# When the third pair's raw up weights are loaded in the second half of a gated MLP

## The chip, the cores and the metric

The kernel runs on one core of a Trainium2 chip. The metric is the device time of one execution in microseconds. The core has five engines that run their own instruction streams and meet through semaphores: TensorE (PE, with PEld for the loading of its weights), VectorE (DVE), ScalarE (ACT), GpSimd (POOL) and SyncE (SP), which here only issues transfers.

## The reference

One decoder layer on 2048 tokens of width 1024: conditioning, two kinds of attention, an output projection, a gated MLP with a causal convolution of width 3, and a final norm. The change touches the up projection of the MLP alone:

```python
h = rms_norm(x, g_mlp[l]) * (1.0 + scale_m) + shift_m
u = causal_depthwise_conv(h @ w_up[l], conv_w[l], conv_b[l])
u_gate, u_val = jnp.split(u, 2, axis=-1)
x = x + gate_m * ((jax.nn.silu(u_gate) * u_val) @ w_down[l])
```

`w_up` is 1024 x 5504 (2752 columns for the gate, 2752 for the value), all in float32.

## The kernel before

**Products.** Each float32 operand is split into a high part, rounded to float32r by ScalarE, and the rest, subtracted by VectorE or GpSimd (`split`, lines 44 to 46). A product is three matmuls: high by high, high by rest, rest by high (`product`, line 1313; its matmuls are recorded at L1315). Products are besides arranged in a fast scheme with seven products in place of eight for a 2 x 2 block product, so operands of h and of the weights are first combined by additions and subtractions.

**Halves and pairs.** The 2048 tokens are worked in two halves of 1024 (`sblk` 0 and 1). In each half the loop goes over 21 pairs of column blocks (128 columns of the gate and the same 128 of the value), and then over a rest of 64 and 64 columns. The first half takes the pairs in the order 0 to 20, the second in the order 2, 3, 0, 1, 4, 5 and so on. So the third pair of the second half is pair 0. The seven finished weights of pairs 2 and 3 were stored in the first half (`wus`), and the second half reads them back (`w_reload`, line 1248; L1251); the other pairs are made anew from the raw weights.

**h.** The second half needs its own operands of h. `load_h` (line 1164, L1167) reads each of four blocks j into a tile `xh`; `h_operands` (line 1169) makes seven operands of it, `op0` to `op6`, with VectorE subtracting (L1192, L1193, L1198, L1199) and `split` making the parts (L45 on ScalarE, L46 on VectorE). The seventh needs a scratch tile `t4` (L1199). The last of all, `obs[NK - 1][6]` with NK = 4, lies in a tile of its own, `op_s`. For the second half they are made while the first half's rest and the second half's first pair are running.

**Raw weights.** `load_pair` (line 1226) fetches the gate and the value columns of one pair from `w_up` into one tile of `raws()` (line 1208), two transfers of 512 KB on SP's queue (L1214). `w_operands` (line 1233) makes seven weights of it: GpSimd makes two combinations in tiles `ws` and one in place (L1237, L1238, L1239), and later a fourth in place (L1246); each is then split into a tile `wu` (L45, L46). The first weight needs no combination, the second needs L1239's.

**Buffers.** `raws()` and the tiles `xh` are allocated from the same three buffers (tag "xh"). `ws` and `t4` share three buffers (tag "ws"); `wu` has seven; accumulators, `snap`, `y` and `u` have their own small rings. A tile gets a buffer when its first instruction is ready and a buffer is free.

**The loop.** At step n the loop (from line 1469) asks for the raw weights of the pair two steps ahead (line 1471), takes the generator that makes the next pair's weights (`weights`, line 1465), and runs seven products over four blocks: 84 matmuls, in `pair_first` (line 1326) at n = 0 and in `pair` (line 1346) after that. `end_pair` (line 1431) then convolves the pair's two tiles `y` into `u` (`conv_tile`, line 1376), gates them and stores the result (`store_g`, line 1404). Two pairs 2k and 2k + 1 share a block `gs[k]`: the odd one's values are added there, by a transfer that accumulates (L1420, on GpSimd's queue), onto what the even one stored (L1415, L1416).

**What sets the order.** The kernel is written in a tile framework. It adds all semaphores, and a planner (`schedule_with_timeline_sim=True`) orders the instructions of each engine and queue ahead of time by its own estimate of when each is ready, with the order of the program as priority. In the stages of attention and output projection the kernel fixes parts of this order by hand (`fixed`, `issue_after`); in the loop of the up projection it doesn't.

Of the kernel before, what the change touches and what calls it, by code (L numbers as in the profile page):

```python
# [34 lines left out]
def kernel(ctx: ExitStack, tc: tile.TileContext, x, c, w_ada, b_ada, g_attn, w_in, b_fgate,  # L35
                      g_out_fox, g_out_sb, w_out, g_mlp, w_up, conv_w, conv_b, w_down, g_final, out):
    nc = tc.nc
# [3 lines left out]
    def f(t):  # L41
        return t.bitcast(F32)
# [62 lines left out]
    def drain(g):  # L105
        for _ in g:
            pass
# [116 lines left out]
    for r, src in ((R_GA, g_attn), (R_GM, g_mlp), (R_GF, g_out_fox), (R_GS, g_out_sb), (R_BA, b_ada)):  # L224
        n = src.shape[1] // P
# [600 lines left out]
    def attend_steps(u):  # L826
        kind, p, tb = u
        if kind == "fox":
            return sum(2 * (2 + 2 * tb + j2 + 1) for j2 in range(2)) + 1
        return sum(2 * (tb + 1 + 2 * tb + j2 + 1) for j2 in range(2)) + 1  # L830
# [199 lines left out]
    for i, u in enumerate(units):  # L1030
# [10 lines left out]
        n = attend_steps(u)  # L1041
# [34 lines left out]
    def chunk(u, c):  # L1076
        t, n, q = ORDER.get(u, TURN)[c]
        if (t, n) not in banks:
            banks[t, n] = bank(psc, "bc", 2) if u == 1 and t == 0 else bank(psd, "o", 4)
        with fixed():  # L1080
            out_matmuls(u, banks[t, n], t, n, q)
        return t, n, q
# [78 lines left out]
    NK = KT // 2  # L1161
    xhs = {}

    def load_h(sblk, j):
        xhs[j] = ho.tile([P, 2, SB], F32, name="xh", bufs=3)
        for i in range(2):
            nc.sync.dma_start(xhs[j][:, i], hms[sblk][:, j + i * NK])  # L1167

    def h_operands(j, sub):
        xh = xhs[j]  # L1170
        tt = ho.tile([P, 2, TB], F32, name="tt", bufs=1)
        t4 = wp.tile([P, TB], F32, name="t4", tag="ws", bufs=3)
        b11, b12 = xh[:, 0, 0:TB], xh[:, 0, TB:SB]
        b21, b22 = xh[:, 1, 0:TB], xh[:, 1, TB:SB]
        ops = obs[j] = [None] * 7

        def put(s, src):
            if j == 0:
                t = ho.tile([P, 2, TB], F32R, name=f"op{s}")
            elif j == NK - 1 and s == 6:  # L1180
                t = spare.tile([P, 2, TB], F32R, name="op_s")
            else:
                t = big4("op")
            split(t[:, 0], t[:, 1], src, nc.vector)
            ops[s] = t

        put(0, b11)
        yield
        put(2, b21)
        put(5, b22)  # L1190
        yield
        sub.tensor_sub(tt[:, 0], b22, b12)  # L1192
        sub.tensor_sub(b12, b12, b11)  # L1193
        yield
        put(4, tt[:, 0])
        put(3, b12)
        yield
        nc.vector.tensor_sub(tt[:, 1], b22, b12)  # L1198
        nc.vector.tensor_sub(t4, b21, tt[:, 1])  # L1199
        yield  # L1200
        put(1, tt[:, 1])
        yield
        put(6, t4)
        yield

    obs = {}

    def raws():
        return ho.tile([P, 2, KT, P], F32, name="wuraw", tag="xh", bufs=3)

    def load_up(raw, col_sets):
        at = 0
        for col, n in col_sets:
            nc.sync.dma_start(raw[:, :, at:at + n], w_up[:, col:col + n].rearrange("(k p) n -> p k n", p=P))  # L1214
            at += n
        return raw

    def w_split(s):
        w = w_tile()
        split(w[:, 0], w[:, 1], s, nc.vector)  # L1220
        return w

    def load_part(t, ci, v):
        return load_up(t[:, v], [(v * DFF + ci * P, P)])

    def load_pair(ci):
        t = raws()
        return load_part(t, ci, 0), load_part(t, ci, 1)

    def w_tile():  # L1230
# [2 lines left out]
    def w_operands(g, v, save=None):  # L1233
        a11, a12, a21, a22 = g[:, 0:NK], g[:, NK:KT], v[:, 0:NK], v[:, NK:KT]
        s3 = wp.tile([P, NK, P], F32, name="ws", tag="ws", bufs=3)
        s2 = wp.tile([P, NK, P], F32, name="ws", tag="ws", bufs=3)
        nc.gpsimd.tensor_sub(s3, a11, a21)  # L1237
        nc.gpsimd.tensor_add(a21, a21, a22)  # L1238
        nc.gpsimd.tensor_sub(s2, a21, a11)  # L1239
        for i, a in enumerate((a11, s2, a12, a21, s3, a12, a22)):  # L1240
            w = w_split(a)
            if save is not None:
                nc.sync.dma_start(wus[save][i], f(w).rearrange("p a k n -> p a (k n)"))
            yield w
            if i == 2:
                nc.gpsimd.tensor_sub(a12, a12, s2)  # L1246

    def w_reload(ci):
        for t in wus[ci]:
            w = w_tile()  # L1250
            nc.sync.dma_start(f(w).rearrange("p a k n -> p a (k n)"), t)  # L1251
            yield w
# [43 lines left out]
    for u in range(1, NU):  # L1296
        for c in range(8 if u == 1 else 0, 16):
            t, n, q = chunk(u, c)
# [22 lines left out]
    def y_tile():  # L1321
        return up_.tile([P, SB + 2], F32, name="y", bufs=3)
# [3 lines left out]
    def pair_first(ws, yg, yv, after):  # L1326

        banks = [bank(psd, "o", 4), bank(psd, "o", 4), bank(psd, "o", 4), bank(psd, "o", 4),
                 bank(psd, "t", 2), bank(psd, "t", 2), bank(psc, "bc", 2)]
        for j in range(NK):  # L1330
            for s in (1, 4, 6, 0, 2, 5, 3):
                product(banks[s], ws[s], obs[j][s], j, j == 0, j == NK - 1)
            if after is not None:
                after(j)
        b1, b6, b2, b5, b7, b3, b4 = banks
        p1, t, u3 = snap(), snap(), snap()
        nc.scalar.activation(p1, b1, AF.Copy)
        nc.vector.tensor_add(t, b6, p1)
        nc.vector.tensor_add(yg[:, T0], b2, p1)
        nc.vector.tensor_add(u3, b7, t)  # L1340
        nc.vector.tensor_add(t, b5, t)
        nc.vector.tensor_add(yv[:, T1], b5, u3)
        nc.vector.tensor_add(yg[:, T1], b3, t)
        nc.vector.tensor_add(yv[:, T0], b4, u3)
# [101 lines left out]
    soon, held = [], []  # L1446
    for sblk, order in enumerate(orders):
        after = None
        if sblk == 0:
            for j in range(1, NK):  # L1450
                if j == NK - 1:
                    load_h(0, j)
                drain(h_operands(j, nc.vector))
            ws = first["ws"]
            after = finish_last
            soon.append(load_pair(1))
        else:
            for j in range(NK):
                if j:
                    load_h(1, j)  # L1460
                drain(h_operands(j, nc.vector))
            for fn in held:
                fn()

        def weights(n):
            ci = order[n]
            return w_reload(ci) if sblk and ci in SAVE else w_operands(*soon.pop(0), ci if ci in SAVE else None)

        for n, ci in enumerate(order):
            if n + 2 < NFULL and not (sblk and order[n + 2] in SAVE):  # L1470
                soon.append(load_pair(order[n + 2]))
            if n == NFULL - 2:
                raw = load_up(raws()[:, 0], [(NFULL * P, REST), (DFF + NFULL * P, REST)])
            last_pair = n == NFULL - 1
            if not last_pair:
                nxt = weights(n + 1)
            elif sblk == 0:
                load_h(1, 0)
                back = w_reload(SAVE[0])
                nxt = islice(back, 5)  # L1480
            else:
                nxt = None
            yg, yv = y_tile(), y_tile()
            if n == 0:
                pair_first(ws, yg, yv, after)
                ws = list(nxt)
            else:
                ws = pair(ws, nxt, yg, yv)
            if last_pair and sblk == 0:
                held.append(lambda yg=yg, yv=yv, ci=ci: end_pair(ci, 0, yg, yv))  # L1490
            else:
                end_pair(ci, sblk, yg, yv)
        w1, w2 = w_split(raw[:, 0:NK]), w_split(raw[:, NK:KT])
        y = y_tile()
        a, b = bank_a(), bank_a()
        oa = [[obs[j][s] for s in (0, 2, 5, 3)] for j in range(NK)]
        for j in range(NK):
            product(a, w1, oa[j][0], j, j == 0, j == NK - 1)
        p1 = snap()
        nc.scalar.activation(p1, a, AF.Copy)  # L1500
        for j in range(NK):
            product(b, w1, oa[j][3], j, j == 0, False)
        for j in range(NK):
            product(a, w2, oa[j][1], j, False, j == NK - 1)
        nc.scalar.activation(y[:, T0], a, AF.Copy)
        for j in range(NK):
            product(b, w2, oa[j][2], j, False, j == NK - 1)
        nc.vector.tensor_add(y[:, T1], b, p1)
        if sblk == 0:
            held.append(lambda y=y: end_rest(y, 0))  # L1510
            ws = ws + list(back)
        else:
            end_rest(y, 1)
# [14 lines left out]
    for kp in range(PRE):  # L1528
        if kp % 2 == 0:
            pre = ho.tile([P, 2, 2, TB], F32, name="pre", tag="xh", bufs=3)  # L1530
        t = pre[:, kp % 2]
# [153 lines left out]
    for i in range(7):  # L1685
        nxt = {}
        kept = []
        for s in range(2):
# [4 lines left out]
            if left:  # L1693
                half, n = lefts[i]
# [68 lines left out]
```

## Time and profile before

| | us |
|---|---|
| runs | 2942.23, 2947.29, 2953.07 |
| median | 2947.29 |
| profiled execution, its time | 2943.39 |
| profiled execution, its span | 2941.4 |
| TensorE busy in the span | 2867.8 |
| granted clock, mean | 0.993 |

The span goes from the first instruction to the last. "Busy" is the time in which an engine works on an instruction; TensorE's instructions overlap, and their ends are modelled. The views used below are: busy time of each engine by stretches; who waited for whom; and the order of time, in which a row has its start, its length, engine, line, operation, tiles written and read, shapes, how many instructions were merged in it, and in brackets the engine's idle time before it and what ended that. For SP a row is the issue of transfers, not their landing. The second half of the up projection runs from about 2104 to 2495 us.

### The profile page before, as it was taken

Reading aid. Unit: us, or ns where it says so; the run is one execution under the profiler, and the core shown is the slowest. Engines: PE = TensorE matmul, PEld = TensorE weight load, DVE = VectorE, ACT = ScalarE, POOL = GpSimd, SP = SyncE. Lnnn points to the kernel's source line nnn. Section 1 sums busy time; section 2 is a strip of 40 time slices with the busy share of each in tenths; the row PEclk is TensorE's granted clock in tenths of the full one; section 3 lists DMA queues with packets and bytes.
Section 4 is the critical chain, followed back from the end, with each engine's and each line's share of the span. In section 5 each row is a group of like instructions: output and inputs, shape, how many; then the busy total and the mean of one; then the engine's idle time right before and its main releaser. Section 6 shows DMA issues by size and latency. Waiting matters only on the chain.

```text
span 2941.4 us, 45922 instructions
## 1 busy us (share of the span) xinstructions
PE 2867.8 (97%) x15772; PEld 2459.7 (84%) x15772; DVE 2179.5 (74%) x3464; ACT 1686.0 (57%) x3187; POOL 901.1 (31%) x967
## 2 busy tenths in 40 slices
PE   8999999999999999999999999999999999999998
PEld 7888888888988988888888788888788888888887
DVE  5787778877886656658843788888998888575476
ACT  5776767677776656658744554444444445433342
POOL 0431322243032423231213344444254543142200
PEclk8999999999999999999999999999999999999999
DMA  9749756867469794794537775554754444975644
GB/s 293 255 139 321 236 188 207 301 211 229 162 212 356 269 277 139 232 323 140 182 120 233 245 232 128 130 136 129 236 132 125 130 130 132 309 257 185 216 158 151
DMA packets 348346, 601.89 MB, mean 205 GB/s; under 512 B 34672, under 2 KB 178800, under 8 KB 348112
## 3 DMA queue, kind: packets, MB, share of 16 engines
q1 hardware_dynamic: 324208, 558.06, 57.7%
q0 software_dynamic: 10880, 20.97, 4.3%
q10 hardware_dynamic: 13024, 19.93, 1.9%
q8 instruction: 124, 2.03, 0.3%
q14 instruction: 110, 0.90, 0.1%
HBM read 420.77 MB, written 177.02 MB: 203 GB/s over the span
## 4 chain that ended last, share of the span: by engine, by line
PE 46%; DMA 3%; DVE 2%; SPq 1%; ACT 1%; issue 1%; POOL 0%; DVEq 0%; ACTq 0%; POOLq 0%
PE ps_o L1315 19%; PE ps_t L1315 7%; PE ps_o L1614 6%; PE ps_t L1614 3%; PE ps_bc L1614 3%; PE ps_o L912 1%; PE ps_pv L615 1%; DMA r<-rstd 1%; PE ps_bc L912 1%; PE ps_pt L606 1%; PE ps_o L1609 1%; DMA wo<-wos 1%; DMA hm<-hf_m 1%; SPq L895 1%; DVE op L46 1%
## 5 line engine op out<-in xcount | busy, mean ns | idle before, releaser
L1315 PE MATMUL ps_o<-op,wu 128*128 128x512 f32 x2592 | 608.0, 389 | 2.0 <-DVE snap L1366 1.5
L1315 PEld LDWEIGHTS ps_o<-op,wu 128*128 128x128 f32 x2592 | 486.2, 188 | 103.9 <-DVE snap L1366 1.9
L611 DVE TENSOR_TENSOR at<-ps_pt,at 128x512 fp32r<-128x512 f32 (+1 forms) x576 | 366.1, 652 | 100.2 <-ACT at L610 97.3
L636 DVE TENSOR_TENSOR_SCAN a<-r,a 128x512 f32<-128x512 f32 (+2 forms) x320 | 368.3, 1167 | 77.8 <-ACT a L631 39.9
L342 PE MATMUL ps_pj<-hp,w_qk 128*128 128x512 f32 x1512 | 411.2, 403 | 14.5 <-DMA hp<-hs 12.9
L610 ACT ACTIVATE at<-ps_pt 128x512 fp32r<-128x512 f32 (+1 forms) x576 | 318.5, 576 | 139.1 <-PE ps_pt L606 123.1
L615 PE MATMUL ps_pv<-at,V 128*128 128x256 f32 x2216 | 386.8, 292 | 9.3 <-DVE at L611 4.2
L615 PEld LDWEIGHTS ps_pv<-at,V 128*128 128x128 f32 x2216 | 320.9, 190 | 39.8 <-DVE at L611 11.4
L342 PEld LDWEIGHTS ps_pj<-hp,w_qk 128*128 128x128 f32 x1512 | 275.4, 190 | 71.0 <-DMA hp<-hs 16.2
L45 ACT ACTIVATE wu<-wuraw 128x512 fp32r<-128x512 f32 x204 | 128.9, 632 | 248.5 <-PE ps_o L1315 190.1
L596 PE MATMUL ps_qk<-K,Q 128*128 128x512 f32 (+2 forms) x640 | 265.7, 416 | 5.6 <-ACT a L631 3.3
L413 PE MATMUL ps_pj<-w_v,hp 128*128 128x256 f32 (+1 forms) x1536 | 236.6, 288 | 2.1 <-DVE hp L422 1.6
L597 PE MATMUL ps_qk<-K,Q 128*128 128x512 f32 (+2 forms) x640 | 235.7, 369 | 0.0
L1315 PE MATMUL ps_t<-op,wu 128*128 128x512 f32 x888 | 220.8, 390 | 1.0 <-DVE op L46 1.0
L413 PEld LDWEIGHTS ps_pj<-w_v,hp 128*128 128x128 f32 x1536 | 209.0, 189 | 10.9 <-DVE q L373 1.5
L630 ACT ACTIVATE r<-ps_qk 128x512 f32<-128x512 f32 (+2 forms) x320 | 173.1, 541 | 58.2 <-PE ps_qk L597 55.5
L46 DVE TENSOR_TENSOR wu<-wuraw,wu 128x512 fp32r<-128x512 f32 x204 | 189.6, 930 | 18.1 <-ACT wu L45 16.7
L1315 PEld LDWEIGHTS ps_t<-op,wu 128*128 128x128 f32 x888 | 166.4, 188 | 36.5 <-DVE op L46 1.8
L606 PE MATMUL ps_pt<-edge,a 128*128 128x128 f32 x1088 | 185.1, 274 | 8.4 <-DVE a L636 7.8
L1614 PE MATMUL ps_o<-op 128*128 128x512 f32 x840 | 191.5, 389 | 0.0
L1614 PEld LDWEIGHTS ps_o<-op 128*128 128x128 f32 x840 | 157.7, 188 | 32.7
L679 ACT ACTIVATE p<-p,mn 128x128 f32<-128x128 f32 (+15 forms) x128 | 153.9, 1203 | 53.3 <-DVE mn L675 52.2
(342 smaller groups left out, 5237.6 us busy)
## 6 DMA issues: line engine op xcount, KB each, us to landing
hp<-hs SPq DMA_DIRECT2D x224, 512.0 KB
wuraw<-in_w_up_dram SPq DMA_DIRECT2D x80, 512.0 KB
ra<-g SPq DMA_DIRECT2D x136, 256.0 KB
rb<-in_w_down_dram SPq DMA_DIRECT2D x108, 256.0 KB
g<-u SPq DMA_DIRECT2D x80, 256.0 KB
hs<-hp SPq DMA_DIRECT2D x32, 512.0 KB
hp<-in_w_ada_dram SPq DMA_DIRECT2D x32, 512.0 KB
qk_fox<-q SPq DMA_DIRECT2D x32, 512.0 KB
```

The source lines that it names most:

```text
L46: (lo_engine or nc.gpsimd).tensor_sub(lo, src, f(hi))
L342: nc.tensor.matmul(acc, w[kt][:, a, n], h[:, bb], start=kt == 0 and i == 0, stop=kt == KT - 1 and i == 2)
L413: nc.tensor.matmul(av[:, t * width:(t + 1) * width], hts[kt][:, a, tok], w[1][kt][:, bb, 0:width], start=kt == 0 and m == 0, stop=kt == KT ...
L596: nc.tensor.matmul(b[:, :cw], Q[:, hl, 0, qcols], K[:, hl, :cw], start=True, stop=False)
L597: marks.append(nc.tensor.matmul(b[:, :cw], Q[:, hl, 1, qcols], K[:, hl, :cw], start=False, stop=True).ins)
L606: nc.tensor.transpose(b[:, i * P:(i + 1) * P], blk(kts[kk], qi), ident)
L610: copies = [nc.scalar.activation(at[:, 0, lo:], b[:, lo:], AF.Copy).ins, nc.vector.tensor_sub(at[:, 1, lo:], b[:, lo:], f(at[:, 0, lo:])).ins]
L611: nc.vector.tensor_sub(at[:, 1, lo:], b[:, lo:], f(at[:, 0, lo:])).ins]
L615: m = nc.tensor.matmul(o[:, 0:2 * P], V[kt // 4][:, kt % 4, hl, :], rhs, start=first and kk == 0 and w == 0, stop=last and kk == 1 and w == 1)
L636: nc.vector.tensor_tensor_scan(rev, r[:, 0:need][:, ::-1], rev, 0.0 if right[qi] is None else right[qi][:, 0:1], ALU.mult, ALU.add)
L1315: nc.tensor.matmul(b, w[:, p, j], o[:, q], start=first and i == 0, stop=last and i == 2, skip_group_check=True)
L1614: nc.tensor.matmul(b, a[:, p, t * P:(t + 1) * P], w[:, q], start=first and i == 0, stop=last and i == 2, skip_group_check=True)
```

## The change

`load_pair` gets a second argument. Where it is given, GpSimd first copies 128 x 2 numbers, the first of the operand's high and of its low part in each partition, into the raw weights' tile, onto the first number of the gate's and of the value's part; the transfers that follow write over them. Since the copy reads the operand and the transfers overwrite what it wrote, the transfers wait for the copy, and the copy waits for the operand. The loop gives the argument at the first step of the second half alone, where the third pair (pair 0) is asked for, and the operand is `op_s`, the last of h. Nothing that is computed changes.

```diff
-    def load_pair(ci):
+    def load_pair(ci, after=None):
         t = raws()
+        if after is not None:
+            nc.gpsimd.tensor_copy(t[:, :, 0, 0:1], f(after[:, :, 0:1]))
         return load_part(t, ci, 0), load_part(t, ci, 1)
...
             if n + 2 < NFULL and not (sblk and order[n + 2] in SAVE):
-                soon.append(load_pair(order[n + 2]))
+                soon.append(load_pair(order[n + 2], obs[NK - 1][6] if sblk and n == 0 else None))
```

## The prediction

> **What bounds the kernel now.** I read four views in this order: the page's table of engines, the busy time of each engine by stretches around the start of the second half, TensorE's waits there, and then the order of time of each engine and queue in the same 60 us.
>
> ```profile
> span 2941.4 us, 45922 instructions
> PE 2867.8 (97%) x15772; PEld 2459.7 (84%) x15772; DVE 2179.5 (74%) x3464; ACT 1686.0 (57%) x3187; POOL 901.1 (31%) x967
> ```
> ```profile
> 2100.00:2120.00 20.00, 18.58 (x80) 14.45 (x79) 19.93 (x25) 10.39 (x17) 6.35 (x5) 1.00 0.71 219
> 2120.00:2140.00 20.00, 19.96 (x88) 16.15 (x87) 16.65 (x22) 8.07 (x12) 6.68 (x6) 1.00 0.62 205
> 2140.00:2160.00 20.00, 20.00 (x90) 16.54 (x89) 18.70 (x23) 9.43 (x14) 8.97 (x8) 1.00 0.38 119
> 2160.00:2180.00 20.00, 20.00 (x90) 16.57 (x89) 20.00 (x24) 9.13 (x13) 11.65 (x9) 1.00 0.78 198
> ...
> 2400.00:2500.00 100.00, 100.00 (x443) 82.80 (x442) 84.91 (x103) 48.12 (x67) 38.66 (x31) 1.00 0.44 126
> ...
> 2800.00:2941.40 141.40, 130.82 (x578) 108.03 (x576) 98.12 (x183) 50.62 (x114) 0.00 (x0) 0.98 0.46 154
> ```
>
> Behind the stretch come PE, PEld, DVE, ACT and POOL busy, then clock, DMA share and GB/s. TensorE sets the time: 2867.8 of 2941.4 us. The change can act from about 2104 us on, where the second half's third pair is loaded. There TensorE is idle for 1.42 us (20.00 less 18.58), then full; the next idle time of size is 10.6 us at the very end (141.40 less 130.82). So 1.42 us is what an edit at this place can win directly.
>
> ```profile
> PE ps_t L1315 <- DVE op L46: 1.0, 1, 1.0
> PE ps_o L1315 <- DVE op L46: 0.5, 1, 0.5
> ```
> ```profile
> 2118.41 0.73 PE L1315 MATMUL ps_t<-op,wu 128*128 128x512 f32 x2 [0.95 <-DVE op L46]
> 2119.62 6.88 PE L1315 MATMUL ps_o<-op,wu 128*128 128x512 f32 x29 [0.47 <-DVE op L46]
> 2126.33 0.84 PE L1315 MATMUL ps_bc<-op_s,wu 128*128 128x512 f32 x3
> 2127.22 0.73 PE L1315 MATMUL ps_o<-op,wu 128*128 128x512 f32 x2
> 2127.79 2.91 PE L1315 MATMUL ps_t<-op,wu 128*128 128x512 f32 x12
> ```
>
> Both waits (0.95 and 0.47 us) are for operands of h that VectorE makes. What holds VectorE up shows when its rows are laid beside GpSimd's.
>
> ```profile
> 2101.10 1.28 DVE L1386 SCALAR_TENSOR_TENSOR u<-y,conv,u 128x1024 f32<-128x1024 f32 x1
> ...
> 2107.72 0.69 DVE L46 TENSOR_TENSOR op<-tt,op 128x512 fp32r<-128x512 f32 x1
> ...
> 2112.66 2.32 DVE L1386 SCALAR_TENSOR_TENSOR u<-y,conv,u 128x1024 f32<-128x1024 f32 x1
> 2114.90 1.78 DVE L46 TENSOR_TENSOR op<-xh,op 128x512 fp32r<-128x512 f32 x1
> 2116.60 1.76 DVE L46 TENSOR_TENSOR op<-tt,op 128x512 fp32r<-128x512 f32 x1
> ...
> 2122.91 0.69 DVE L46 TENSOR_TENSOR op_s<-t,op_s 128x512 fp32r<-128x512 f32 x1
> ```
> ```profile
> 2107.26 1.18 POOL L1381 COPY halo<-y 128x2 f32<-128x2 f32 x1 [11.97 <-DVE y L1508]
> ...
> 2112.61 1.28 POOL L1237 TENSOR_TENSOR ws<-wuraw 128x512 f32<-128x512 f32 x1 [4.04 <-DMA wuraw<-in_w_up_dram]
> 2113.97 2.16 POOL L1238 TENSOR_TENSOR wuraw<-wuraw 128x512 f32<-128x512 f32 x1
> 2116.21 1.61 POOL L1239 TENSOR_TENSOR ws<-wuraw 128x512 f32<-128x512 f32 x1
> 2123.68 1.29 POOL L1237 TENSOR_TENSOR ws<-wuraw 128x512 f32<-128x512 f32 x1 [5.87 <-DVE op_s L46]
> ...
> 2126.28 0.19 POOL L1378 COPY y<-halo 128x2 f32<-128x2 f32 x1
> ```
>
> While GpSimd does the third pair's three combinations (1.28 + 2.16 + 1.61 = 5.05 us), three VectorE instructions take 2.32, 1.78 and 1.76 us, against 1.28 and 0.69 undisturbed: 1.04 + 1.09 + 1.07 = **3.2 us of delay** just before the operands for which TensorE waits. op_s is complete at 2123.60 (2122.91 + 0.69).
>
> **The change, part by part.** The loads concerned, on SP's queue, and the first use of the third pair's weights:
>
> ```profile
> 2104.82 1.01 SPq L1214 DMA_DIRECT2D wuraw<-in_w_up_dram  x2
> ...
> 2107.87 2.99 SPq L1214 DMA_DIRECT2D wuraw<-in_w_up_dram  x2
> 2116.09 4.61 SPq L1251 DMA_DIRECT2D wu<-wus  x5
> ...
> 2122.24 1.42 SPq L1214 DMA_DIRECT2D wuraw<-in_w_up_dram  x2
> 2123.75 4.83 SPq L1251 DMA_DIRECT2D wu<-wus  x2
> ```
> ```profile
> 2126.53 0.63 ACT L45 ACTIVATE wu<-wuraw 128x512 fp32r<-128x512 f32 x1 [3.65 <-PE ps_o L1315]
> ...
> 2127.21 0.30 PEld L1315 LDWEIGHTS ps_o<-op,wu 128*128 128x128 f32 x2 [0.46 <-ACT wu L45]
> ```
> ```profile
> 2130.69 10.43 PE ps_o L1315 x46
> ```
>
> By the loop's order the three pairs of L1214 loads are those of the third, fourth and fifth pair of the half; the L1251 loads bring the second pair's finished weights back. Nothing is removed. **Added** is one GpSimd copy of 128 x 2 numbers: the same shape costs 0.19 to 1.18 us here. GpSimd is idle 13.3 of 20 us between 2120 and 2140 (6.68 busy), so it lies beside other work; without that cover it delays at most the instruction behind it, a fourth pair's combination, by 1.2 us.
>
> **Moved** are two loads of 512 KB and what hangs on them. Load to first use took 2112.61 - 2104.82 = 7.8 us. If the loads keep their buffer and merely wait, they start at 2123.60 + 0.6 = 2124.2, GpSimd begins at 2132.0, and its three instructions end at 2137.0. The first weight needs no combination: its split (0.63 + 0.69 us, as the ACT and VectorE rows) is done at 2133.3; the second, made of the last combination, at 2138.3. When does TensorE need them? A matmul takes 10.43/46 = 0.227 us. After 2127.2 at least 84 - 29 = 55 matmuls of the second pair are left (the x29 row cannot hold more of it): 12.5 us, so the need is at 2139.7, and for the second weight 12 matmuls later, at 2142.4. Margins: 6.4 and 4.1 us. What is late next is the two matmuls at 2127.22, which are already of the third pair and fill a gap: without them TensorE waits from 2127.2 to 2127.8, 0.6 us. The 1 MB that now stands in the busiest stretch costs 1.05 MB / 205 GB/s = 5.1 us to whatever is behind it, at worst 1.0 us beyond the second weight's margin. So, if the change does what it says: at best **-1.4 us** (both waits gone), with the filler gone -0.8, and from the other side -1.42 + 1.42 (waits unchanged) + 0.6 + 1.0 + 1.2 = **+2.8 us**. I take -0.8, since the margins hold.
>
> The rows say that one engine's instruction stretches beside the other's by about 1 us each. [...]
>
> **But does it do that?** The wait is tied to a buffer, not to GpSimd. Three buffers are shared by the loads of h and the raw weights, and they fall free at 2104.82, 2107.87 and 2122.24, all before op_s. Nothing in the code keeps the fourth pair's load from the buffer that the third leaves, and the order of this loop is the planner's, which takes what is ready: that third pair's matmuls stand at 2127.22, amid the second's, shows it. Then the fourth pair is loaded at 2104.82, finds the same two free buffers for its combinations (now its L1237 at 2123.68 waited for the one under op_s), and the same three instructions meet VectorE at 2112.6. The pairs have changed places, and the stall of 1.42 us stays. I hold this likeliest: **no change, +0 to +1.2 us** for the copy.
>
> The profiled execution took 2943.39 us (2941.4 of span and 2.0 around it), 3.9 below the median of 2947.29; all sums are differences, so forecast and rivals are put on the median: 2947.3 + 0 gives **2947**.
>
> **The rivals.**
>
> *It does what it says* (chance 0.24): the buffer is kept for the third pair. For it: VectorE's 3.2 us lie directly ahead of the stall. Against it: the free buffer. 2947.3 - 0.8 = 2946.5.
>
> *The wait takes its place in a queue* (0.10): SP holds the delayed load ahead of the five L1251 loads of 2116.09. They would start at 2124.2 and land, by the 7.8 us of the L1214 loads, at 2132.0, where TensorE has work of the first pair only until 2123.5 (if 12 of the x29 row are the second pair's first product, 17 are the first's: 2119.62 + 17 x 0.227): 8.5 us, 2955.8. Against it: SP now puts the loads of 2107.87 ahead of these reloads although they belong to a later pair, so queues are filled by readiness.
>
> *The third pair is left out in the cold* (0.22, the slower side): fourth, fifth and sixth pair take all three buffers before op_s is made, the third gets one only when a pair is used up, and its load competes with each later one. The fourth pair's gated product must then wait in its buffer (of three) for the third's sums, since the two share a block of g. Price: a pair whose raw weights come without lead costs load, combinations and split: 7.8 + 5.05 + 1.3 = 14.2 us. Now the third pair has a lead of 2127.21 - 2104.82 = 22.4 us; it decides once a lead falls under 14.2. One such pair gives 2961.5, two 2975.7. For it: VectorE has no reserve to catch up at once (20.00 of 20.00 in 2160 to 2180). Against it: TensorE is full from 2127 on even after that squeeze.
>
> *A luckier order* (0.04): the 10.6 us at the end shrink with the 1.42. Even all of both is 12.0 us, 2935; for over 14.7 us something would be needed that no row here shows.
>
> **How the numbers follow.** The forecast has 0.40. A measurement here can tell about 0.5%, 14.7 us, from no change. Forecast, does-as-it-says and queue (0.40 + 0.24 + 0.10) stay within that: 0.74. The cold third pair, 14.2 to 28.4 us, I count whole to slower: 0.22; the lucky order, generously, to faster: 0.04. The forecast's own range is the runs' scatter (2942.23 to 2953.07) with -1.4 and +2.8: 2941 to 2956. The range for 8 in 10 reaches to one lost lead and the scatter above it, 2961.5 + 5.8 = 2967, and 2 us lower than the scatter: 2939.
>
> **What would show it.** Right: in 2104 to 2128 TensorE again idles about 1.4 us behind L46 making op, three GpSimd instructions L1237 to L1239 stand before op_s, and the L1214 loads at about 2105 and 2108 are still there, with another pair's columns; the new copy stands on GpSimd after op_s. The rival is right if GpSimd is free of L1237 to L1239 from 2110 to op_s and the VectorE rows read 1.28 and 0.69. The queue shows as L1251 loads after the copy; the cold pair as TensorE idle for 5 us or more behind wu after 2130. Wrong altogether I am if TensorE's idle time after 2130 grows by over 15 us, or if its idle time before 2100 changes.

## The result, and the profile after

The changed kernel took 2952.11 us in the median of 20 runs (2948.12 to 2959.85); the kernel before, run beside it, 2947.84 (2942.12 to 2953.48, 20 runs). The medians differ by 4.3 us. The ratio is 1.0017 with a 95% interval of 1.0009 to 1.0025: by it about 5.0 us slower, between 2.7 and 7.4. That is less than 0.5%, but "no change" lies outside the interval. The profiled execution took 2955.03 us, 11.6 more than the profiled one of before, so more than half of that difference must be scatter, and the first question is where it arose.

**A measure for that.** Both traces hold 15772 TensorE matmuls. I subtract the start of the n-th matmul of the one from that of the n-th of the other and call the difference the lag (worked out from the trace's records). From the 10800th matmul to the 12000th, before the first instruction that the change touches, the lag of the changed kernel is constant at 6.80 us: scatter of the earlier stages. At the 12090th (2093.2 us in the trace of before) it is 6.88, at the 12270th 5.96, at the 12300th 11.34, and from the 12420th to the end 11.76. What the change does is what the lag gains from the 12090th to the 12600th (2211.5 us): **+4.9 us**, of one execution, against +5.0 by the timed ratio. It falls into a small gain, -0.9 us, and a loss of 5.8 us some 20 us later. In the rows of after everything behind line 1226 stands two lines lower (L1315 is now L1317), and 7 us are to be taken off their times to lay them beside those of before.

The gain first. VectorE and GpSimd ahead of op_s, and then GpSimd's next rows, after the change (in order of time):

```profile
2119.00 1.28 DVE L1388 SCALAR_TENSOR_TENSOR u<-y,conv,u 128x1024 f32<-128x1024 f32 x1
2120.20 0.68 DVE L46 TENSOR_TENSOR op<-xh,op 128x512 fp32r<-128x512 f32 x1
2120.80 0.68 DVE L46 TENSOR_TENSOR op<-tt,op 128x512 fp32r<-128x512 f32 x1
...
2126.03 0.69 DVE L46 TENSOR_TENSOR op_s<-t,op_s 128x512 fp32r<-128x512 f32 x1
```
```profile
2126.78 0.19 POOL L1229 COPY wuraw<-op_s 128x2 f32<-128x2 f32 x1 [11.87 <-DVE op_s L46]
2126.90 0.19 POOL L1380 COPY y<-halo 128x2 f32<-128x2 f32 x1
2139.11 1.29 POOL L1239 TENSOR_TENSOR ws<-wuraw 128x512 f32<-128x512 f32 x1 [12.02 <-DMA wuraw<-in_w_up_dram]
2140.48 2.15 POOL L1240 TENSOR_TENSOR wuraw<-wuraw 128x512 f32<-128x512 f32 x1
2142.71 2.14 POOL L1241 TENSOR_TENSOR ws<-wuraw 128x512 f32<-128x512 f32 x1
2144.81 2.26 POOL L1239 TENSOR_TENSOR ws<-wuraw 128x512 f32<-128x512 f32 x1
```

The three VectorE rows that read 2.32, 1.78 and 1.76 us now read 1.28, 0.68 and 0.68: GpSimd is idle for 11.87 us ahead of the copy, so the collision is gone from here. op_s is complete at 2126.72, aligned at 2119.8 instead of 2123.6. So the combinations are out of VectorE's way, as the change intended. TensorE's waits, grouped by what ended them, from 2080 to 2520 us (total, times, longest), and its rows in order of time:

```profile
PE ps_o L1317 <- DVE snap L1368: 2.5, 2, 1.5
PE ps_o L1317 <- DMA wu<-wus: 1.4, 1, 1.4
PE ps_o L1317 <- ACT wu L45: 1.2, 1, 1.2
PE ps_t L1317 <- ACT wu L45: 0.8, 1, 0.8
```
```profile
2126.59 6.21 PE L1317 MATMUL ps_o<-op,wu 128*128 128x512 f32 x26 [1.39 <-DMA wu<-wus]
...
2141.48 2.88 PE L1317 MATMUL ps_o<-op,wu 128*128 128x512 f32 x12
2145.57 0.73 PE L1317 MATMUL ps_o<-op,wu 128*128 128x512 f32 x2 [1.21 <-ACT wu L45]
2147.13 0.73 PE L1317 MATMUL ps_t<-op,wu 128*128 128x512 f32 x2 [0.83 <-ACT wu L45]
2148.80 8.19 PE L1317 MATMUL ps_o<-op,wu 128*128 128x512 f32 x28 [0.94 <-DVE snap L1368]
```

No wait for op is left. In its place, almost at the same spot, stands 1.39 us for the second pair's first stored weight: it had been hidden behind the wait for h. The small gain is the difference. Measured from the start of one matmul to the next, less 0.227 us, before lost 2.55 us here: 1.98 in the two waits for op, 0.26 just ahead of them, 0.31 at the third pair's two matmuls at 2127.22. The changed kernel loses 1.66 us, all at the reload. (The longer of the two waits for snap, 1.5 us, lies at about 2090 and is in both kernels.) Then come three waits that before did not have, 1.21 + 0.83 + 0.94 = 2.98 us, for weights of the third pair and for a VectorE instruction. Measured in the same way they cost 1.48 + 1.10 + 1.11 = 3.7 us. The rest of the loss is in the last row: 28 matmuls in 8.19 us, where 28 x 0.227 + 0.17 makes 6.5. The busy time of the engines by short stretches there (PE, PEld, DVE, ACT, POOL, then clock, DMA share, GB/s) shows why:

```profile
2145.30:2148.70 3.40, 1.47 (x4) 0.59 (x4) 3.40 (x4) 3.20 (x6) 3.40 (x3) 1.00 0.12 47
2148.70:2152.10 3.40, 3.30 (x8) 2.62 (x9) 3.40 (x5) 0.00 (x0) 2.76 (x3) 0.50 0.00 0
2152.10:2155.50 3.40, 3.40 (x17) 2.79 (x16) 3.40 (x4) 1.27 (x2) 2.71 (x3) 1.00 0.02 5
```

In the stretch with the waits TensorE is busy for 1.47 of 3.40 us; in the next its granted clock is 0.50, and 8 matmuls start instead of 17. The trace's record of the clock has this half rate from 2148.7 us on for 3.41 us, which costs 1.7. So 3.7 + 1.7 = 5.4 us of the 5.8 are named; the other 0.4 us are lost in one place, at 2173.6.

**Why the weights were late.** The issues on SP's queue, and ScalarE, which splits the weights:

```profile
2113.01 0.32 SPq L1409 DMA_DIRECT2D gl<-u  x1
2122.97 2.48 SPq L1253 DMA_DIRECT2D wu<-wus  x5
2125.54 0.94 SPq L1445 DMA_DIRECT2D gl<-u  x1
2126.53 7.04 SPq L1214 DMA_DIRECT2D wuraw<-in_w_up_dram  x3
2133.97 1.27 SPq L1253 DMA_DIRECT2D wu<-wus  x1
2135.29 4.78 SPq L1214 DMA_DIRECT2D wuraw<-in_w_up_dram  x3
```
```profile
2137.33 0.63 ACT L45 ACTIVATE wu<-wuraw 128x512 fp32r<-128x512 f32 x1 [7.06 <-DMA wuraw<-in_w_up_dram]
...
2144.88 0.63 ACT L45 ACTIVATE wu<-ws 128x512 fp32r<-128x512 f32 x1 [4.17 <-POOL ws L1241]
```

All six transfers of raw weights, two each for the third, fourth and fifth pair, now stand behind the five reloads, the first of which SP could not issue before 2122.97. The row of 2126.53 merges three transfers. By the trace's records the first, at 2126.53, starts 0.25 us before the copy, so it is not one of the third pair's. Those are issued at 2127.45 and 2129.71: ScalarE's first split at 2137.33 starts when the one lands, GpSimd's first combination at 2139.11 when the other does. (The expectation of e11 below counts 12.6 us from 2126.53; from the third pair's own first issue it is 11.7.) What this did to the transfers is seen in two stretches of before and the same two of after, aligned:

```profile
2097.00:2119.00 22.00, 21.05 (x92) 16.60 (x90) 21.97 (x28) 12.76 (x22) 6.35 (x5) 1.00 0.75 226
2119.00:2139.00 20.00, 19.49 (x85) 15.64 (x85) 16.62 (x22) 7.70 (x11) 6.68 (x6) 1.00 0.67 220
```
```profile
2104.00:2126.00 22.00, 21.20 (x94) 17.24 (x92) 21.84 (x32) 13.38 (x22) 1.31 (x2) 1.00 0.37 132
2126.00:2146.00 20.00, 18.20 (x79) 14.67 (x79) 12.14 (x13) 5.10 (x8) 7.04 (x6) 1.00 1.08 321
```

(132 - 226) x 22 us is -2.07 MB, (321 - 220) x 20 us is +2.02 MB: two pairs, not one, moved from the first stretch into the second, where the second pair's reloads already stood. There the DMA share goes to 1.08 (above 1 since the packets' recorded times overlap: by the trace's records up to 25 packets at once, where the share counts 16 engines). Issue to first combination is now 2139.11 - 2127.45 = 11.7 us, instead of 7.8. And when the loads land, GpSimd has third and fourth pair to combine back to back, beside VectorE's convolution. Before and after:

```profile
2133.01 3.98 DVE L1385 SCALAR_TENSOR_TENSOR u<-y,conv,u 128x1024 f32<-128x1024 f32 x2 [0.72 <-ACT u L1383]
2136.91 1.27 DVE L1386 SCALAR_TENSOR_TENSOR u<-y,conv,u 128x1024 f32<-128x1024 f32 x1
...
2138.71 1.28 DVE L1386 SCALAR_TENSOR_TENSOR u<-y,conv,u 128x1024 f32<-128x1024 f32 x1
```
```profile
2139.61 4.10 DVE L1387 SCALAR_TENSOR_TENSOR u<-y,conv,u 128x1024 f32<-128x1024 f32 x2 [0.93 <-ACT u L1385]
2143.63 4.51 DVE L1388 SCALAR_TENSOR_TENSOR u<-y,conv,u 128x1024 f32<-128x1024 f32 x2
2148.07 0.68 DVE L1368 TENSOR_TENSOR snap<-ps_o,snap 128x512 f32<-128x512 f32 x1
```

The four instructions take 8.61 us. Undisturbed ones of this shape take 1.28 each, 5.12 in all, but the same four already took 6.53 before the change, beside other work of GpSimd's. So 2.1 us of delay are new, two thirds of the 3.2 that the collision ahead of op_s had cost, and behind them is the snap for which TensorE waits.

### The profile page after: what moved, and what is told of

It is laid out like the page before. It is cut to its first block, busy times and chain, and to the rows that moved or that the text cites. A ratio compares the mean times of both kernels' runs of the same rounds, so it can differ in the third digit from the quotient of the medians.

```text
span 2953.2 us, 45917 instructions
## 1 busy us (share of the span) xinstructions
PE 2872.7 (97%) x15772; PEld 2462.3 (83%) x15772; DVE 2175.9 (74%) x3464; ACT 1685.6 (57%) x3187; POOL 904.1 (31%) x968
## 4 chain that ended last, share of the span: by engine, by line
PE 47%; DVE 3%; DMA 2%; ACT 1%; issue 1%; SPq 0%; POOL 0%; DVEq 0%; ACTq 0%; POOLq 0%
PE ps_o L1317 18%; PE ps_t L1317 7%; PE ps_o L1616 6%; PE ps_t L1616 3%; PE ps_bc L1616 3%; PE ps_o L912 3%; PE ps_pv L615 1%; PE ps_pt L606 1%; PE ps_bc L912 1%; DMA r<-rstd 1%; PE ps_o L1611 1%; PE ps_qk L596 1%; PE ps_qk L597 1%; DMA hm<-hf_m 0%; DVE u L1387 0%
## 5 line engine op out<-in xcount | busy, mean ns | idle before, releaser
L1317 PE MATMUL ps_o<-op,wu 128*128 128x512 f32 x2592 | 610.3, 390 | 5.1 <-DVE snap L1368 2.5
L1317 PEld LDWEIGHTS ps_o<-op,wu 128*128 128x128 f32 x2592 | 487.1, 188 | 107.9 <-DVE snap L1368 3.3
L615 PEld LDWEIGHTS ps_pv<-at,V 128*128 128x128 f32 x2216 | 321.5, 190 | 42.4 <-DVE at L611 11.6
L1317 PE MATMUL ps_t<-op,wu 128*128 128x512 f32 x888 | 220.9, 390 | 0.9 <-ACT wu L45 0.8
L1317 PEld LDWEIGHTS ps_t<-op,wu 128*128 128x128 f32 x888 | 166.3, 188 | 36.6 <-ACT wu L45 1.3
```

Of the source, the lines that this page charges most:

```text
L615: m = nc.tensor.matmul(o[:, 0:2 * P], V[kt // 4][:, kt % 4, hl, :], rhs, start=first and kk == 0 and w == 0, stop=last and kk == 1 and w == 1)
L1317: nc.tensor.matmul(b, w[:, p, j], o[:, q], start=first and i == 0, stop=last and i == 2, skip_group_check=True)
```

## The experiments

Twelve kernels, among them the changed one unaltered (e7). "Gain" is the lag gained between the 12090th and the 12600th matmul of one profiled execution. Ratios with an interval are timed against the kernel before on the same chip; its medians there were 2948.64, 2947.54 and 2948.47 us.

| kernel | gain, us | half clock | timed ratio, or one time |
|---|---|---|---|
| after | +4.9 | 3.41 us | 1.0017 [1.0009, 1.0025] |
| e7, the same again | +5.9 | 3.41 | 1.0022 [1.0009, 1.0035] |
| e1, the copy alone | +0.6 | none | 1.0003 [0.9989, 1.0017] |
| e2, combinations wait, loads early | -0.1 | none | 1.0001 [0.9990, 1.0012] |
| e3, fourth pair asked for first | +6.5 | 6.83 | 1.0015 [1.0001, 1.0030] |
| e4, fourth pair waits instead | +0.9 | none | 2949.78 |
| e5, waits for op0 instead of op_s | +3.2 | 3.41 | 2949.81 |
| e6, copy by ScalarE | +6.1 | 6.83 | 2950.62 |
| e8, only the value part waits | +2.7 | none | 2955.18 |
| e9, before, eight buffers wu | -2.3 | none | 0.9997 [0.9981, 1.0013] |
| e10, e2 and eight buffers wu | -2.3 | none | 0.9998 [0.9986, 1.0009] |
| e11, third pair's loads on ScalarE's queue | +7.1 | 6.83 | 2956.44 |
| e12, after and eight buffers wu | +1.8 | 3.41 | 1.0018 [1.0007, 1.0029] |

The two executions of the changed kernel differ by 1.0 us in the gain, so differences of that size tell nothing. A half clock costs half its length (8 matmuls instead of 17 in the 3.40 us of after, 1.7 us); without it the gains of after, e7, e3 and e6 are 3.2, 4.2, 3.1 and 2.7 us. My theory was that the moved loads cost the time: the third pair's weights come late, through transfers that collide with the reloads, and TensorE waits for them. The rivals: the copy itself, the later combinations, the other pairs' loads, GpSimd's queue.

**The copy alone (e1).** The tile is touched by the copy, but with a source that is ready long before.

```diff
-            nc.gpsimd.tensor_copy(t[:, :, 0, 0:1], f(after[:, :, 0:1]))
+            nc.gpsimd.tensor_copy(t[:, :, 0, 0:1], ones[:, 0:2].rearrange("p (a b) -> p a b", b=1))
...
-                soon.append(load_pair(order[n + 2], obs[NK - 1][6] if sblk and n == 0 else None))
+                soon.append(load_pair(order[n + 2], sblk and n == 0 or None))
```

> The copy into the third pair's tile stays on GpSimd, but takes its numbers from a constant, so that it waits for the buffer alone and not for h. Theory (the late loads cost): the loads are back at about 2105, the lag is 0 within 0.5 us, and TensorE's 1.4 us of waiting for op is there again. Rival (the copy, as one more instruction and one more step ahead of the transfer, costs): +1 us or more.

The waits of before are back, and by timed runs the time is that of before. The gain of 0.6 us is a little above the 0.5 that I had allowed, but under my +1 for the rival: the copy is at most a small part of the loss.

```profile
PE ps_t L1317 <- DVE op L46: 1.0, 1, 1.0
PE ps_o L1317 <- DVE op L46: 0.5, 1, 0.5
PE ps_o L1317 <- DVE op_s L46: 0.4, 1, 0.4
```

**Late combinations, early loads (e2).** On the kernel before, the copy now writes the first scratch tile of the third pair's combinations, so that these wait for op_s while the loads do not.

```diff
-    def w_operands(g, v, save=None):
+    def w_operands(g, v, save=None, after=None):
...
+        if after is not None:
+            nc.gpsimd.tensor_copy(s3[:, 0, 0:2], f(after[:, 0, 0:2]))
         nc.gpsimd.tensor_sub(s3, a11, a21)
...
-            return w_reload(ci) if sblk and ci in SAVE else w_operands(*soon.pop(0), ci if ci in SAVE else None)
+            return w_reload(ci) if sblk and ci in SAVE else w_operands(
+                *soon.pop(0), ci if ci in SAVE else None, obs[NK - 1][6] if sblk and n == 2 else None)
```

> The raw weights are loaded as before the change. The wait for the last operand of h is put on GpSimd's first combination of the third pair instead (a copy of two columns from op_s into the tile that this combination writes). So the combinations come after h, as the change has it, and the loads do not. Theory (late loads are the cost): L1237 to L1239 leave the stretch before op_s, both waits for op go, the second pair's run covers the combinations, and the lag is -1.4 to 0 us. Rival (the cost is GpSimd's combinations meeting VectorE after h, whatever the loads do): +2 us or more.

The collision ahead of op_s is gone here too, and the loss is not there. GpSimd does the combinations right behind op_s, at 1.28 us each, while VectorE is idle for 6.25 us:

```profile
2122.91 1.28 POOL L1239 TENSOR_TENSOR ws<-wuraw 128x512 f32<-128x512 f32 x1
```
```profile
2129.02 0.69 DVE L1340 TENSOR_TENSOR snap<-ps_o,snap 128x512 f32<-128x512 f32 x1 [6.25 <-PE ps_o L1317]
```

But there is no gain either: the waits for h have turned into waits for the reloads, as at the head of the changed kernel (1.6 us in two):

```profile
PE ps_o L1317 <- DMA wu<-wus: 1.6, 2, 1.3
```

**The fourth pair asked for first (e3).** This makes what my forecast had thought would happen: the fourth pair gets the first free buffer.

```diff
-            if n + 2 < NFULL and not (sblk and order[n + 2] in SAVE):
-                soon.append(load_pair(order[n + 2], obs[NK - 1][6] if sblk and n == 0 else None))
+            if sblk and n == 0:
+                fourth = load_pair(order[3])
+                soon += [load_pair(order[2], obs[NK - 1][6]), fourth]
+            elif n + 2 < NFULL and not (sblk and (n == 1 or order[n + 2] in SAVE)):
+                soon.append(load_pair(order[n + 2]))
```

> As changed, but the fourth pair's raw weights are asked for ahead of the third's, so the fourth loads at about 2105 and only the third and what is asked after it wait for op_s. Theory A (the third pair's own lateness costs, the others are only queued behind it): the lag stays at +3 to +5 us. Theory B (three loads of 1 MB in a row after op_s cost, each slowing the other): with one of them gone the lag falls to +2 us or less. Theory C (the fourth pair's combinations now take the stretch that the third's left): TensorE's 1.4 us of waiting for op come back on top, +5 us or more.

Now one pair is loaded early, as its L1214 row at 2111.84 shows (7.6 us to be taken off here):

```profile
2111.84 1.01 SPq L1214 DMA_DIRECT2D wuraw<-in_w_up_dram  x2
...
2127.11 8.11 SPq L1214 DMA_DIRECT2D wuraw<-in_w_up_dram  x3
```

It did not bring the time of before. The third pair's loads and weights were as late as in the changed kernel (combined from 2140.82 on, TensorE waiting 2.2 us and 0.8 us for wu), and the gain is no smaller. At 6.5 us it lies above theory A's range; 3.4 us of it are half clock. Theory C's sign, waits for op, is not there: the fourth pair's combinations did not come early with its load, GpSimd makes none before 2140.82.

**The fourth pair waits, the third does not (e4).** The condition `n == 0` becomes `n == 1`.

> The wait for op_s is put on the fourth pair's load instead of the third's; the third loads at about 2105 as before, the fourth and fifth after op_s. Theory (what costs is that the third pair, the next that TensorE needs, has no lead): the third's combinations stand at 2112 again, TensorE's waits for op are there again (1.4 us), and as the fourth is needed 19 us later its lateness costs nothing: lag 0 to +0.8 us. Rival (any two loads of raw weights behind the five reloads cost): +2.5 us or more.

The expected waits for op did not come back; what is left is 1.3 us for a reload and 1.1 for snap, and a gain of 0.9, a little above the range. The third pair's combinations do start ahead of op_s again, but here GpSimd loses:

```profile
2117.05 1.28 DVE L1388 SCALAR_TENSOR_TENSOR u<-y,conv,u 128x1024 f32<-128x1024 f32 x1
```
```profile
2117.68 4.20 POOL L1239 TENSOR_TENSOR ws<-wuraw 128x512 f32<-128x512 f32 x1 [4.72 <-DMA wuraw<-in_w_up_dram]
```

In the kernel before, GpSimd's first combination started 0.05 us ahead of this VectorE instruction (2112.61 against 2112.66), which then took 2.32 us. Here it starts 0.63 us behind, takes 4.20 us itself instead of 1.28, and VectorE's row and the four behind it (0.69 each) are undisturbed. The next two (64x512, 0.69 each in e2) take 1.67 and 1.75 us.

So lateness of the fourth and later pairs is nearly free. With e3 this says: what costs is that the *third* pair comes late.

**The copy by another engine (e6).** If the copy blocked GpSimd's queue, ScalarE would free it.

```diff
-            nc.gpsimd.tensor_copy(t[:, :, 0, 0:1], f(after[:, :, 0:1]))
+            nc.scalar.activation(t[:, :, 0, 0:1], f(after[:, :, 0:1]), AF.Copy)
```

> As changed, but ScalarE makes the copy. Theory (the load's start counts, not who starts it): GpSimd is free, all else stays, lag +4 to +6 us with TensorE's waits for wu as in the changed kernel. Rival (GpSimd's in-order queue, held by the waiting copy for 12 us, costs): lag under +2 us.

The loss stays (+6.1, at the upper end of the range; TensorE waits 3.7 us for wu in one piece). GpSimd's queue is not the cause.

**Waiting for less (e5, e8).** In e5 the copy reads op0 of the last block instead of op_s; in e8 it touches the value part alone, so that the gate part loads early.

> As changed, but the load waits for the first operand of h's last block (obs[3][0]) instead of the last. By the changed kernel's rows that operand is made about 8 us before op_s, so the loads start at about 2117 to 2118 ahead of the five reloads of the second pair's weights. Theory (the cost is the third pair's lateness): lag 0 to +2 us. Rival A (the cost is the order of transfers): the reloads now stand behind 2 MB of raw weights, TensorE waits for wu from wus by 3 us or more, lag +3 us or more. Rival B (any wait of a load on h costs the same): +5 us.

> As changed, but the copy writes onto the value's half of the tile alone, so that only the value's transfer waits for h; the gate's is issued at about 2105. The third pair's first weight (gate columns only) is then ready early, while the three combinations are as late as in the changed kernel. Theory (TensorE waits for the combined weights, the second onward, because their load is late): the first weight's split no longer waits for a load, but TensorE's waits for wu remain, lag +2 to +5 us. Rival (it is the first split, stuck at the head of ScalarE's queue for 7 us ahead of the evictions, that costs): lag under +1.5 us.

e5 is mixed. The copy ran at 2116.09, the combinations began at 2123.88, and TensorE waited 1.9 us for op and 1.8 us for a reload, but not for wu. From start to start it loses 4.2 us in these waits and 1.6 in its half clock, which begins at their end, against 2.55 us here in before: that is its gain of 3.2, but of neither theory's making. e8 has about half of the changed kernel's gain, with 2.0 us for reloads and 1.2 for wu, and the clock is never halved. That is in the theory's range: TensorE waits for the combined weights though the first split, at 2136.04, waits for no load. Single executions are all I have of both.

**Another queue (e11).** If SP's queue held the loads back, ScalarE's would let them land in the 7.8 us of before.

```diff
...
-        return load_part(t, ci, 0), load_part(t, ci, 1)
+        queue = nc.scalar if after is not None else None
+        return load_part(t, ci, 0, queue), load_part(t, ci, 1, queue)
```

> As changed, but the third pair's two transfers are issued on ScalarE's queue, so that they do not stand behind the five reloads of 512 KB that SP issued just before. In the changed kernel GpSimd could begin 12.6 us after the issue (2126.53 to 2139.11), where the prediction took 7.8. Theory (the queue ahead of the load makes the difference): GpSimd begins 8 to 9.5 us after the issue, and the lag falls to +1 to +3 us. Rival (the transfers share the same engines and the reloads are only slowed in turn): GpSimd begins 11 us or more after the issue, or the second pair's reloads come late instead, and the lag stays at +4 or more.

SP's queue and ScalarE's issue, and GpSimd makes the copy and its first row behind the load:

```profile
2124.60 1.26 SPq L1214 DMA_DIRECT2D wuraw<-in_w_up_dram  x1
```
```profile
2125.35 1.69 ACTq L1214 DMA_DIRECT2D wuraw<-in_w_up_dram  x2
```
```profile
2125.13 0.19 POOL L1229 COPY wuraw<-op_s 128x2 f32<-128x2 f32 x1 [11.87 <-DVE op_s L46]
...
2141.84 1.82 POOL L1240 TENSOR_TENSOR ws<-wuraw 128x512 f32<-128x512 f32 x1 [16.41 <-DMA wuraw<-in_w_up_dram]
```

It takes 16.5 us from issue to combination instead of 11.7, and TensorE waits 5.8 us in one piece. My theory of the queue's order fell. The DMA share from 2122 to 2142 is 1.05, near the 1.08 of the changed kernel, and the transfers from a queue of their own came no sooner: 16.5 us is the rival's sign, 11 us or more.

**Room for the reloads (e9, e10, e12).** If the 1.4 us for a reload is what the removed wait for h turned into, an eighth buffer `wu` must free it: e9 is the kernel before with `bufs=8`, e10 is e2 with it, e12 the changed kernel with it.

> The kernel before with eight buffers for finished weights instead of seven; no wait on h. In the run with the combinations behind h, TensorE's 1.4 us of waiting for op turned into 1.6 us of waiting for the second pair's first reloaded weight, whose buffer falls free late. Here that reload has a buffer early. Theory (two waits one behind the other; this removes the hind one alone): TensorE still waits for op by about 1.4 us, lag -0.3 to +0.3 us. Rival (the planner's new order changes more than that): outside.

> GpSimd's first combination of the third pair waits for op_s (loads early) and eight buffers for finished weights: both waits are attacked. Theory: neither the wait for op nor that for the reload is left, TensorE runs through from 2093 to 2212, lag -1.5 to -0.9 us, the most that can be had here; no timed runs can tell that. Rival (a third wait stands behind these two): -0.5 us or above.

> The changed kernel with eight buffers for finished weights. Eight buffers alone gave -2.3 us, all of TensorE's waiting between 2080 and 2130. Theory (front waits and late third pair are separate costs that add): lag +4.9 - 2.3 = +2.6 us, within 1. Rival A (with TensorE ahead by 2.3 us it meets the late weights earlier and waits that much longer): +4 to +6 us. Rival B (the eighth buffer gives the second pair the lead that hides the third): under +1 us.

In e10 TensorE is full (PE busy is the first of the engines):

```profile
2100.00:2120.00 20.00, 20.00 (x90) 16.57 (x89) 19.94 (x30) 11.69 (x20) 9.60 (x4) 1.00 0.75 210
2120.00:2140.00 20.00, 20.00 (x90) 16.58 (x89) 17.72 (x20) 8.41 (x13) 12.65 (x11) 1.00 0.66 223
```

But so it is in e9, which I had expected within 0.3 us of before: the eighth buffer alone changes the order so that the waits for op go as well, and the wait on h adds nothing to it. Both gains, -2.3, lie below what I had expected. (From the 12000th matmul on, which takes in their reload waits at 2087 to 2093, e9 has -1.9, e10 -2.0 and e12 +2.8.) e12 keeps a loss against e9, 1.8 + 2.3 = 4.1 us, and its timed ratio is no better than the changed kernel's: with room for the reloads the late third pair costs nearly what it costs without. Its one wait of TensorE from 2095 to 2230 is behind VectorE, and its clock is halved after it. So the theory's +2.6 came out within 1, though no wait for wu is in it:

```profile
PE ps_o L1317 <- DVE snap L1364: 2.5, 1, 2.5
```
```profile
2140.00:2160.00 20.00, 19.31 (x86) 15.56 (x84) 18.65 (x18) 6.84 (x12) 15.58 (x11) 1.00 0.68 197
2160.00:2180.00 20.00, 18.24 (x73) 14.89 (x74) 18.08 (x21) 9.87 (x15) 12.86 (x9) 0.91 0.59 135
```

By timed runs e9 and e10 cannot be told from the kernel before; no version here beats it measurably.

## Why the prediction was right or wrong

The forecast of no change was wrong by its sign, though the time lies in its range and under 0.5%.

- **What bounds the kernel, and the collision: right.** TensorE's two waits were behind VectorE's stretched instructions, and these behind GpSimd's three. Where the three went away, in after and in e2, the VectorE rows fell to 1.28 and 0.68 and the waits for h ended. But the overlap alone does not say which engine loses: in e4 it was first GpSimd (4.20 us instead of 1.28), and the waits for h ended too.
- **"The fourth pair is loaded at 2104.82": the step that failed.** I had reckoned that the planner takes what is ready, so that the fourth pair's load passes the waiting third. It wasn't issued there. SP's queue, whose order the planner sets ahead of time, now had the five reloads ahead of all raw loads; SP issued nothing from 2113.01 to 2122.97, and the fourth pair's two transfers came at 2126.53 and 2135.29, just ahead of the third's and behind them. So GpSimd was free ahead of op_s, the sign that I had set down for the rival "it does what it says". That a later request can pass an earlier one was not wrong in itself: in e5 a transfer of raw weights is issued at 2111.76, 4.3 us before the copy, so it belongs to another pair than the third. And e3 shows that the forecast's next step would have failed as well: there the fourth pair is loaded at 2104 aligned, but its three instructions do not meet VectorE ahead of op_s; they stay behind the third pair's. Why the planner ordered SP's queue in this way no view shows.
- **That rival's gain, 0.8 to 1.4 us: mis-sized.** The row that spoke against it was not in my list of what is late next: the reload behind the wait for h. At the front 1.66 us at the reload stand against 2.55 lost before. The net -0.9 is close to my -0.8 by luck. Neither term of that sum came as I had put it: the reload took back most of what the waits for h had cost, and the +0.6 for the missing filler did not come, since TensorE has no gap at that place. In e2, without the late loads, nothing is left of it.
- **Its margins of 6.4 and 4.1 us: mis-sized, and this decides the sign.** I had put 7.8 us for the load; it took 11.7. I moved 1 MB; it was 2 MB, into a stretch whose share rose to 1.08. I had put 5.05 us for the three combinations; they took 2144.85 - 2139.11 = 5.74. op_s came 3.8 us earlier and paid for part: the second weight was split at 2145.51, aligned by the lag of 5.96 at 2139.6, 1.3 us later than the 2138.3 of my sum. But the need came earlier too: the matmul that waited for it is the 12277th, which starts at 2138.24 in before, not 2142.4. Margin +4.1 became -1.3, the wait of 1.2 to 1.4 us that the rows show.
- **The upper bound of +2.8 us: too low,** since no term was in it for a second collision (2.1 us of VectorE's time beyond before) nor for the clock. Of the change's loss of 5.8 us at least 1.7 is a halved clock.
- **What GpSimd's moved work costs VectorE: not in my sum.** The traces differ by what VectorE does there. In e2 it was idle for 6.25 us, and the moved work cost nothing; in after it was convolving, and lost 2.1 us more than before the change, against 3.2 ahead of op_s.
- **The other rivals: fell.** The five reloads were issued at 2122.97, ahead of the raw loads, so they did not queue behind them; the cold pair's 14.2 us did not come, since the second pair's matmuls covered most of the delay. The copy, 0.19 us, was hidden as said.

What stays open: why the planner put the raw loads behind the reloads; why in e5, where op0 is awaited, the wait for op grows to 1.9 us; and what part of the transfers' 11.7 us is waiting behind the reloads and what part is sharing with them.

## What to carry to other kernels

Delaying a load to keep an engine out of another's way moves three things: the collision, the bytes, and, where a planner sets the order, other loads of the same queue. Price the load at the traffic of the stretch into which it goes, not at that from which it comes (here 11.7 us, not 7.8), and ask what will be late next at the place where the wait is removed: here the next wait was 1.39 us behind one of 1.42. When the aim is the engines' collision alone, delay the instructions and leave the load early (e2 lost nothing, though it gained nothing either).

## What the runs showed of the hardware

I had not expected a halved clock behind three waits of about 1 us each. Of the eight kernels in which the third pair's loads wait (after, e3, e5, e6, e7, e8, e11, e12) seven have a stretch of half clock, always 3.41 or 6.83 us long; the kernels with the early load (before, e1, e2, e4, e9, e10) have none in this stretch. In the records of before and after every stretch at one rate, full or half, is a multiple of 3.41 us long, but for the last, which ends with the record. In after TensorE was busy for 1.47 of the 3.40 us ahead of the drop, with no single wait above 1.21 us.

The length of a single wait does not decide it. e12 has one of 2.7 us at 2092 without a drop and one of 2.5 us, ahead of 2161.76, with one. What fits, with one overlap, is the share of a window. I divided the fourteen traces, from about 2082 to 2235 us, into windows of 3.41 us that continue the record of the clock. In the windows ahead of the seven drops TensorE was busy for 0.03 to 0.45 of the time; in every other window at full clock for 0.45 or more (0.45 in e10, 0.49 in e9, 0.50 in e12, in the rest 0.55 and above). At 0.45 the share alone does not tell the two apart, and elsewhere it can mislead: ahead of the half clock at 158.75 us of after TensorE was busy for 2.58 of 3.41 us, 0.76. e12's wait of 2.7 us fell across two windows, busy for 0.50 and 0.72. So waits that are short each, but close together, were paid for once more: here with 1.7 us on 3.7.
